# One of four weight sums on VectorE, fills begun several tasks ahead, first loads through one queue

## The chip, the core and the metric

The kernel runs on one core of one Trainium2 chip. Its time is device microseconds (us) of that core from launch to end. The kernel before was timed three times: 1735.0, 1737.59 and 1738.17 us, so the median is 1737.59 us. A further execution was taken with the hardware profiler; all rows in this document come from such executions.

The engines are named as in the profile: PE is TensorE's matrix multiply and PEld its weight load, DVE is VectorE, ACT is ScalarE, POOL is GpSimd, SP is the sync engine, which only issues DMAs here. ACT and POOL issue DMAs too.

## What is computed

One layer of a hybrid block on a sequence of 512 positions with 2048 channels, all in float32. Cut to what matters:

```
h = rmsnorm(x, norm_g)                       # (512, 2048)
proj = h @ w_in                              # (2048, 15360) weights: ten parts
a_u, a_b, a_c, a_z, b_v, b_g, b_z, c_u, c_z, gates = split(proj)
y_a = (silu(a_z) * a_b * conv3(a_c * a_u)) @ w_br_a
v   = conv31(b_v * sigmoid(b_g)) + conv_b    # causal, per channel, 31 taps
y_b = (silu(b_z) * silu(layernorm(v))) @ w_br_b
y_c = (silu(c_z) * (group(meanpool(c_u) - c_u) * scale)) @ w_br_c
merged = sigmoid(g0) * y_a + sigmoid(g1) * y_b + sigmoid(g2) * y_c
out = rmsnorm(x + merged @ w_o, final_g)
```

## The kernel before

**The product with w_in is done in 15 units.** A unit is a pair of 512-column blocks of `w_in`. Its two operands are cut in two by rows (channels 0-1023 and 1024-2047), in two by columns (the pair) and in two by positions (0-255 and 256-511), and the two-by-two block product is made with seven half-size products in place of eight. They are named `11`, `12`, `s1`, `s4`, `s2`, `s3`, `22`, in this order (the table `PRODUCTS`). Each of the seven has four *stages* of one weight block, 128 partitions x 1024 columns, 512 KB; so a unit has 28 stages and reads 28 blocks, 14 MB, of the 16 blocks of `w_in` that it uses. Every float32 number is split in a high part (`wh` for weights, made by ACT, L132) and a low part (`wl`, made by DVE, L133), and a product takes three matmuls: high x high, high x low, low x high.

**The weights of the seven products are sums.** In a unit, tile `rawA` of a stage is loaded with block (0,0) for `11`; for `s1` block (0,1) is added to it in place; for `s2` block (1,1) is added; for `22` block (1,0) is added. Tile `rawB` is loaded with block (1,0) for `12`; another `rawB` is loaded with block (1,1) for `s4`, and for `s3` block (0,1) is added to it. In the kernel before, each addition is an accumulating DMA that POOL issues (`accum_op`, L113): it reads the block from device memory and adds it to the tile. It waits until DVE has made `wl` of the tile's earlier content. Plain loads are issued by SP (L109). There are four `rawA` and six `rawB` tiles, so a plain load waits until the tile's earlier content has been split. The class `Weights` runs this: `next()` hands the matmuls a split block, `split_to` splits two stages ahead of them, `load_to` issues loads up to four stages ahead of the split.

**Other work is a list of tasks.** Vector work (31-tap convolution, layer norm, pooling, gates) is put in `todo` with a cost for each task; after the matmuls of every half stage (a step) `feed()` runs tasks until a credit of `rate` per step is used up. Results that are needed only later are spilled to device memory by a DMA that ACT issues (`spill`) and brought back by one that SP issues (`fill`); before the change most fills are tasks of cost 0 that stand one task, or a few, ahead of their use. Spilled and filled tiles, and nearly every temporary, share one pool of 20 buffers of 256 KB (`tp`). The recorded program is then put in an order for each engine by a scheduler that goes by its own timeline; the weight splits have a high priority in it (`AHEAD`).

**The start.** `x` is needed twice: transposed (`xT`, in 16 tiles of 128 x 2 x 256 floats) as the matmul operand, and by rows (`xn`, 16 tiles) for the sums of squares of the norm. The eight `xT` tiles of positions 0-255 (`xa` and `x12`) are loaded by DMAs that ACT issues, the eight of positions 256-511 by SP, in the steps of unit 0. Each `xn` tile is loaded by SP and squared by ACT in one call (`square`).

**The last part.** After the 15 units, the three branch products (w_br) and the product with `w_o` run in plain form: 80 more weight blocks with one load each.

The functions that the change touches, and what calls them, with the profile's line numbers:

Of the kernel before, what the change touches and what calls it, by code (L numbers as in the profile page):

```python
# [9 lines left out]
F32R = mybir.dt.float32r  # L10
AF = mybir.ActivationFunctionType
ALU = mybir.AluOpType
# [6 lines left out]
KB = WB // P  # L19
# [3 lines left out]
CONV_B = 31  # L23
# [5 lines left out]
RAW = 2 * CH  # L29
AHEAD = 300  # L30
WARM = 8


P_G = 0
# [11 lines left out]
for _c in (0, CH):  # L46
# [44 lines left out]
class Weights:  # L91
# [3 lines left out]
    def __init__(self, tc, nc, pools, parts, src, load_ahead, split_ahead):  # L95
        self.tc, self.nc, self.pools, self.parts, self.src = tc, nc, pools, parts, src
        self.load_ahead, self.split_ahead = load_ahead, split_ahead
        self.stages = stages()
        self.last = {s[1]: n for n, s in enumerate(self.stages)}
        self.raw, self.done = {}, {}  # L100
        self.loaded = self.split = self.at = 0

    def load_to(self, n):
        while self.loaded < min(n, len(self.stages)):
            tag, key, what, b = self.stages[self.loaded]
            if what == "load":
                t = self.pools[tag].tile([P, RAW], F32, tag=tag, name=f"raw{tag}{self.loaded}")
                for at in self.pieces(self.loaded):
                    self.nc.sync.dma_start(out=t[:, at], in_=self.src[b][:, at])  # L109
            else:  # L110
                t, before = self.raw[key]
                assert self.split > before
                self.nc.gpsimd.dma_start(out=t, in_=self.src[b], accum_op=ALU.add)  # L113
            self.raw[key] = t, self.loaded
            self.loaded += 1

    def pieces(self, n):
        step = CH if n == 0 else RAW
# [35 lines left out]
def trunk(ctx: ExitStack, tc: tile.TileContext, xT, xn, wts, par, fg, out):  # L154
# [85 lines left out]
    urgent, todo = deque(), deque()  # L240
    rate, credit = [0.5], [0.0]

    def add(cost, f, *args):
        todo.append((cost, lambda: f(*args)))

    def soon(cost, f, *args):
        urgent.append((cost, lambda: f(*args)))

    def feed():
        credit[0] = min(credit[0] + rate[0], 2.0)  # L250
        while credit[0] > 0.0 and (urgent or todo):
            cost, f = (urgent or todo).popleft()
            f()
            credit[0] -= cost

    def flush():
        while urgent or todo:
            (urgent or todo).popleft()[1]()

    def halves(src, t):  # L260

# [84 lines left out]

    squares = const.tile([P, 4 * NT], F32, name="squares")

    def square(t, c):
        x = tmp("xq")  # L350
        nc.sync.dma_start(out=x, in_=xn[t, :, c * CH : (c + 1) * CH])
        A.activation(out=x, in_=x, func=AF.Square, accum_out=squares[:, 4 * t + c : 4 * t + c + 1])

    def roots():
# [132 lines left out]
    def conv_tasks(i):  # L487
# [26 lines left out]
            else:  # L514
                V.tensor_tensor(out=csum[0], in0=csum[0], in1=c, op=ALU.add)

        return [(0.0, load), (0.5, first)] + [(0.7, lambda s=s: tap(s)) for s in range(1, CONV_B)] + [(0.7, last)]

    def pair_tasks(i):
        for pair in zip(conv_tasks(i), conv_tasks(i + 1)):  # L520
            todo.extend(pair)

    mean, var, rstd, held = {}, {}, {}, {}

# [3 lines left out]
    def center_tasks():  # L528
# [23 lines left out]
            var.clear()  # L552

        add(0.7, average)
        add(0.0, conv_load, 0)
        add(1.0, lambda: None)
        for i in range(KB):
            if i + 1 < KB:
                add(0.0, conv_load, i + 1)
            add(1.4, center, i)  # L560
        add(3.5, spread)

    def act_tasks():
# [19 lines left out]
        add(0.0, load, 0)  # L583
        for i in range(KB):
            if i + 1 < KB:
                add(0.0, load, i + 1)
            add(2.6, act, i)


# [59 lines left out]
    def pool_tasks(gi):  # L649
# [27 lines left out]
            ucd[2 * gi + o] = spill(s, "uc")  # L677

        mean_cost = 2.2 + 0.8 * gi
        add(0.0, load, "cu", cud, 0)  # L680
        add(0.0, load, "cu", cud, 1)
        add(mean_cost, mean_of, 0)
        add(0.0, weights)
        add(mean_cost, mean_of, 1)
        add(0.0, load, "cz", czd, 0)
        add(0.7, weights_split)
        add(0.0, load, "cz", czd, 1)
        add(1.0, lambda: None)
        add(0.7, mix, 0)
        add(0.7, mix, 1)  # L690
        add(0.0, st.clear)


    def halved(d, u, i):
        t = fill(d[i], "u")
        u[i] = halves(t, slot(F32R, "u"))

    def halved_tasks(d, u):
        for i in range(KB):
            add(0.7, halved, d, u, i)  # L700


    gd = [[[None] * 4 for _ in range(NT)] for _ in range(3)]
# [4 lines left out]
    def first_each(n):  # L708
        while makes and KD * len(sets) // 2 - 2 * len(makes) <= n + 4:
            make(*makes.popleft())  # L710
        if n in (2, 4, 6, 8):
            j = n // 2 - 1
            xload(nc.sync, x22[j], j, 1, 1)
            xload(nc.sync, xa[j][:, :, half[1]], j, 0, 1)
        if n == 10:
            nc.sync.dma_start(out=prm, in_=par)
        if n >= 32 and n % 3 == 2:
            square(*squares_left.popleft())

    def second_each(n):  # L720
        if n % 2 == 0 and squares_left:
            square(*squares_left.popleft())
        if n == 18:
            roots()
        if n >= 20 and late:
# [262 lines left out]
```

## Time and profile before

| | us |
|---|---|
| median of three runs | 1737.59 |
| the profiled execution, its own time | 1735.44 |
| its span, first to last instruction | 1733.7 |
| PE busy | 1658.1 |
| DVE busy | 1077.9 |
| ACT busy | 736.7 |
| POOL busy (issuing DMAs included) | 208.3 |
| mean granted TensorE clock, share of full speed | 0.986 |

The profiled execution took 1735.44 us, 1.7 us more than its span; the difference lies before the first and after the last instruction. Matmuls are pipelined, so PE can be busy and still not issue at its best rate: the number of matmuls in a stretch of time, shown in parentheses behind the busy time, says more than the busy time. A matmul of this kernel moves 512 columns, apart from some transposes of 128.

### The profile page before, as it was taken

The page shows a single profiled execution, that of the slowest core. Times are in us where ns is not written, and L with a number is a line of the kernel's source. Part 1 is how long each engine was busy: PE and PEld are TensorE (multiplying, and loading weights), DVE is VectorE, ACT ScalarE, POOL GpSimd, SP SyncE. Part 2 cuts the span into 40 slices and gives each one's busy share as a digit, 9 for nine tenths or more (in the row PEclk, how much of TensorE's full clock was granted, in tenths as well). Part 3 has the DMA queues.
Part 4 walks back from the last instruction along what each step waited for, and adds up shares of the span by engine and source line. Part 5 has one row for each costly group of instructions (what it writes and reads, how often), then busy time and mean ns, then how long its engine had stood idle before and what let it go on. Part 6 is the DMA issues. An engine that isn't in the chain of part 4 may idle for free.

```text
span 1733.7 us, 19754 instructions
## 1 busy us (share of the span) xinstructions
PE 1658.1 (96%) x7332; PEld 1355.1 (78%) x7332; DVE 1077.9 (62%) x1360; ACT 736.7 (42%) x919; POOL 208.3 (12%) x246
## 2 busy tenths in 40 slices
PE   5899999999999999999899989999899999999997
PEld 4677887887878787887687868888688888888887
DVE  5845699599679859756776754545543444553342
ACT  5645543443444454555554544545541211222222
POOL 0202020211112121212021102121200000000000
PEclk9999999999999999999999989999899999999999
DMA  9789897988879897989898989998995544443212
GB/s 314 145 226 208 241 193 183 196 203 200 184 186 201 201 231 177 240 216 277 249 258 244 276 244 210 226 206 245 223 297 184 195 146 146 134 146 92 91 37 97
DMA packets 119504, 345.41 MB, mean 199 GB/s; under 512 B 13168, under 2 KB 17392, under 8 KB 119408
## 3 DMA queue, kind: packets, MB, share of 16 engines
q0 software_dynamic: 34560, 125.84, 39.7%
q1 hardware_dynamic: 61216, 177.40, 31.0%
q10 hardware_dynamic: 23632, 40.91, 6.6%
q8 instruction: 57, 0.93, 0.2%
q14 instruction: 39, 0.32, 0.0%
HBM read 308.45 MB, written 35.65 MB: 198 GB/s over the span
## 4 chain that ended last, share of the span: by engine, by line
PE 83%; DMA 8%; DVE 4%; ACT 2%; issue 1%; SPq 0%; ACTq 0%; DVEq 0%
PE X L379 11%; PE X L380 10%; PE X L381 10%; PE Z L379 5%; PE Z L380 5%; PE Z L381 5%; PE y L816 5%; PE y L815 5%; PE y L814 5%; PE V L380 3%; PE V L379 3%; PE V L381 3%; PE o L888 3%; PE o L890 3%; PE o L889 3%; DVE wl L133 2%
## 5 line engine op out<-in xcount | busy, mean ns | idle before, releaser
L133 DVE TENSOR_TENSOR wl<-rawA,wh 128x1024 fp32r<-128x1024 f32 (+1 forms) x281 | 341.8, 1218 | 251.2 <-ACT wh L132 247.6
L132 ACT CAST wh<-rawA 128x1024 fp32r<-128x1024 f32 (+1 forms) x281 | 294.5, 1049 | 435.6 <-PE X L380 146.2
L133 DVE TENSOR_TENSOR wl<-rawB,wh 128x1024 fp32r<-128x1024 f32 x220 | 268.4, 1222 | 285.5 <-ACT wh L132 284.4
L132 ACT CAST wh<-rawB 128x1024 fp32r<-128x1024 f32 x220 | 231.2, 1053 | 343.8 <-PE y L815 106.5
L113 POOL DMA_DIRECT2D rawA<-wts x180 | 155.7, 865 | 902.8 <-DVE wl L133 865.0
L379 PE MATMUL X<-wh,x 128*128 128x512 f32 x480 | 191.5, 400 | 33.6 <-ACT x L307 17.3
L379 PE MATMUL X<-wh,xs 128*128 128x512 f32 x480 | 192.3, 401 | 20.0 <-ACT wh L132 18.1
L379 PE MATMUL Z<-wh,xs 128*128 128x512 f32 x480 | 189.4, 396 | 6.1 <-ACT wh L132 3.8
L380 PE MATMUL X<-wh,xs 128*128 128x512 f32 x480 | 190.2, 396 | 0.0
L380 PE MATMUL Z<-wh,xs 128*128 128x512 f32 x480 | 188.0, 392 | 2.3 <-DVE xs L300 2.3
L380 PE MATMUL X<-wh,x 128*128 128x512 f32 x480 | 189.7, 395 | 0.0
L381 PE MATMUL X<-wl,x 128*128 128x512 f32 x480 | 179.7, 397 | 0.0
L381 PE MATMUL X<-wl,xs 128*128 128x512 f32 x480 | 175.9, 397 | 3.8 <-DVE wl L133 3.7
L381 PE MATMUL Z<-wl,xs 128*128 128x512 f32 x480 | 174.1, 392 | 0.1
L502 DVE SCALAR_TENSOR_TENSOR conv<-v,prm,conv 128x511 f32<-128x511 f32 (+28 forms) x240 | 165.6, 726 | 0.1
L814 PE MATMUL y<-wh,u 128*128 128x512 f32 x384 | 149.9, 390 | 0.0
L815 PE MATMUL y<-wh,u 128*128 128x512 f32 x384 | 149.7, 390 | 0.0
L816 PE MATMUL y<-wl,u 128*128 128x512 f32 x384 | 149.5, 390 | 0.0
L379 PEld LDWEIGHTS X<-wh,x 128*128 128x128 f32 x480 | 91.7, 191 | 59.2 <-issue 17.7
L379 PEld LDWEIGHTS X<-wh,xs 128*128 128x128 f32 x480 | 91.7, 191 | 46.8 <-ACT wh L132 20.0
L379 PEld LDWEIGHTS Z<-wh,xs 128*128 128x128 f32 x480 | 90.4, 189 | 32.6 <-ACT snap L387 7.2
L381 PEld LDWEIGHTS X<-wl,xs 128*128 128x128 f32 x480 | 91.6, 192 | 25.3 <-DVE wl L133 5.9
(172 smaller groups left out, 2289.3 us busy)
## 6 DMA issues: line engine op xcount, KB each, us to landing
rawA<-wts POOLq DMA_DIRECT2D x180, 512.0 KB, 7.5
rawB<-wts SPq DMA_DIRECT2D x160, 512.0 KB, 5.2
rawA<-wts SPq DMA_DIRECT2D x99, 512.0 KB, 4.1
rawB<-wts POOLq DMA_DIRECT2D x60, 512.0 KB, 7.7
g<-g SPq DMA_DIRECT2D x48, 256.0 KB, 5.2
d<-turn ACTq DMA_DIRECT2D x32, 256.0 KB, 7.0
g<-gate ACTq DMA_DIRECT2D x24, 256.0 KB, 6.0
g<-snap ACTq DMA_DIRECT2D x24, 256.0 KB, 5.6
```

The source lines that it names most:

```text
L113: self.nc.gpsimd.dma_start(out=t, in_=self.src[b], accum_op=ALU.add)
L132: self.nc.scalar.copy(out=h[:, at], in_=raw[:, at])
L133: self.nc.vector.tensor_tensor(out=l[:, at], in0=raw[:, at], in1=h[:, at].bitcast(F32), op=ALU.subtract)
L379: T.matmul(p, lhsT=xh, rhs=h, start=start and k == 0, stop=False, skip_group_check=True)
L380: T.matmul(p, lhsT=xl, rhs=h, start=False, stop=False, skip_group_check=True)
L381: T.matmul(p, lhsT=xh, rhs=l, start=False, stop=k == KB - 1, skip_group_check=True)
L502: V.scalar_tensor_tensor(out=c[:, s:], in0=v[:, : S - s], scalar=pcol(P_BW, i * CONV_B + CONV_B - 1 - s), in1=c[:, s:], op0=ALU.mult, op1= ...
L814: T.matmul(banks[t], lhsT=uh[:, tk], rhs=h, start=k == 0, stop=False)
L815: T.matmul(banks[t], lhsT=ul[:, tk], rhs=h, start=False, stop=False)
L816: T.matmul(banks[t], lhsT=uh[:, tk], rhs=l, start=False, stop=k == KB - 1)
L888: T.matmul(pt[t], lhsT=mh[:, tk], rhs=h, start=k == 0, stop=False)
L889: T.matmul(pt[t], lhsT=ml[:, tk], rhs=h, start=False, stop=False)
```

## The change

1. **The sum for `s2` moves from a DMA to VectorE.** The block that `s2` adds to `rawA`, (1,1), is the one that `s4` has loaded in `rawB`. The entry of `s2` in the table becomes `sum`, and `sum_to` issues a `tensor_tensor` add of the two tiles on DVE, with the priority of the splits. 60 of the 240 accumulating DMAs go, and 60 adds of 128 x 1024 float32 come. The next sum on the `rawB` tile (for `s3`) may start only once the add has read it.
2. **Fills begin ahead.** `before(f)` files a load with the planned cost of the tasks ahead of it, and `begin_loads` starts it when the tasks done are within `LOAD_AHEAD` = 7.0 cost units of it. An empty task of 7.0 units is put behind the layer norm's statistics.
3. **The squares' loads** start two squares ahead of the squaring.
4. **The first loads** all go through SP, weight block and `xT` tile in turn; the second half of `xT` follows at once and is no longer spread over unit 0's steps.

```diff
-    ("s2", "A", "add", 1, 1),
+    ("s2", "A", "sum", 1, 1),
...
     def load_to(self, n):
...
+            if what == "sum":
+                pass
...
+    def sum_to(self, n):
+        while self.summed < min(n, len(self.stages)):
+            _, key, what, b = self.stages[self.summed]
+            if what == "sum":
+                t, before = self.raw[key]
+                assert self.split > before and self.loaded > self.summed
+                with self.tc.high_priority(AHEAD):
+                    self.nc.vector.tensor_tensor(out=t, in0=t, in1=self.held[b], op=ALU.add)
+                self.raw[key] = t, self.summed
+            self.summed += 1
...
     def split_to(self, n):
         while self.split < min(n, len(self.stages)):
             n_stage = self.split
+            self.load_to(n_stage + 1)
+            self.sum_to(n_stage + 3)
             self.load_to(n_stage + 1 + self.load_ahead)
...
-    w.load_to(1)
     for j in range(STEPS):
-        xload(nc.scalar, xa[j][:, :, half[0]], j, 0, 0)
+        w.load_to(j + 1)
+        xload(nc.sync, xa[j][:, :, half[0]], j, 0, 0)
     for j in range(STEPS):
-        xload(nc.scalar, x12[j], j, 1, 0)
+        w.load_to(STEPS + j + 1)
+        xload(nc.sync, x12[j], j, 1, 0)
+    for j in range(STEPS):
+        xload(nc.sync, x22[j], j, 1, 1)
+        xload(nc.sync, xa[j][:, :, half[1]], j, 0, 1)
...
+    def before(f, *args):
+        loads.append((planned[0], lambda: f(*args)))
...
+    def begin_loads():
+        while not urgent and loads and loads[0][0] <= spent[0] + LOAD_AHEAD:
+            loads.popleft()[1]()
...
-        add(0.0, conv_load, 0)
         add(1.0, lambda: None)
         for i in range(KB):
-            if i + 1 < KB:
-                add(0.0, conv_load, i + 1)
+            before(conv_load, i)
             add(1.4, center, i)
         add(3.5, spread)
+        add(LOAD_AHEAD, lambda: None)
...
-        if n >= 32 and n % 3 == 2:
-            square(*squares_left.popleft())
+        if n >= 24 and n % 3 == 2:
+            square_load()
+            if n >= 32:
+                square(*xqs.popleft())
```

The loads of the convolution's `v`, the activation's `c` and `z`, the pooling's `cu`, `cz` and weights, and the branches' `u` are turned from tasks into `before(...)` in the same way.

How this moves instructions shows at three places. The first is SP's queue at the start; the rows are its loads from the first on, before the change (`rawA0` is stage 0's block, the number behind `raw` is the stage):

```order
L109 DMA rawA0_93<-wts 128x512 x2
L109 DMA rawA1_162<-wts 128x1024
L109 DMA rawA2_164<-wts 128x1024
L109 DMA rawA3_166<-wts 128x1024
L109 DMA rawB4_168<-wts 128x1024
L109 DMA rawB5_176<-wts 128x1024
L109 DMA rawB6_182<-wts 128x1024
L205 DMA xa_1_81<-xT 128x2x256
L205 DMA x22_9_89<-xT 128x2x256
L109 DMA rawB7_207<-wts 128x1024
L205 DMA x22_10_90<-xT 128x2x256
```

and with it:

```order
L113 DMA rawA0_93<-wts 128x512 x2
L228 DMA xa_1_81<-xT 128x2x256
L113 DMA rawA1_97<-wts 128x1024
L228 DMA xa_2_82<-xT 128x2x256
L113 DMA rawA2_100<-wts 128x1024
L228 DMA xa_3_83<-xT 128x2x256
L113 DMA rawA3_103<-wts 128x1024
L228 DMA xa_4_84<-xT 128x2x256
L113 DMA rawB4_106<-wts 128x1024
L228 DMA x12_5_85<-xT 128x2x256
L113 DMA rawB5_109<-wts 128x1024
L228 DMA x12_6_86<-xT 128x2x256
```

The `xT` tiles `xa_1` to `xa_4` and `x12` were on ACT's queue and now stand in SP's, each behind its stage's block; the `x22` tiles and the second halves of `xa`, which began ahead of block 7, moved behind it.

The second is DVE in unit 6, in the product `s1` (stages 176 to 179) and the first stages of `s4` (180 on); `conv` are taps of the convolution, `snap` joins of products. Before:

```order
L133 TENSOR_TENSOR wl177_4030<-rawA169_3751,wh177_4029 128x1024
L502 SCALAR_TENSOR_TENSOR conv_207_3763<-v_205_3747,prm_104,conv_207_3763 128x497
L392 TENSOR_TENSOR snap_220_3965<-V_222_3969,snap_220_3965 128x512
L502 SCALAR_TENSOR_TENSOR conv_206_3749<-v_204_3745,prm_104,conv_206_3749 128x496
L392 TENSOR_TENSOR snap_221_3966<-V_223_3970,snap_221_3966 128x512
L133 TENSOR_TENSOR wl178_4058<-rawA170_3780,wh178_4057 128x1024
L502 SCALAR_TENSOR_TENSOR conv_207_3763<-v_205_3747,prm_104,conv_207_3763 128x496
L502 SCALAR_TENSOR_TENSOR conv_206_3749<-v_204_3745,prm_104,conv_206_3749 128x495
L133 TENSOR_TENSOR wl179_4077<-rawA171_3799,wh179_4076 128x1024
L502 SCALAR_TENSOR_TENSOR conv_207_3763<-v_205_3747,prm_104,conv_207_3763 128x495
L133 TENSOR_TENSOR wl180_4096<-rawB180_4008,wh180_4095 128x1024
```

and with the change, where `rawA168<-rawA168,rawB180` is a sum for `s2`:

```order
L556 SCALAR_TENSOR_TENSOR conv_207_3763<-v_199_3599,prm_126,conv_207_3763 128x497
L446 TENSOR_TENSOR snap_220_3965<-V_222_3969,snap_220_3965 128x512
L446 TENSOR_TENSOR snap_221_3966<-V_223_3970,snap_221_3966 128x512
L134 TENSOR_TENSOR rawA169_3751<-rawA169_3751,rawB181_4027 128x1024
L156 TENSOR_TENSOR wl178_4058<-rawA170_3780,wh178_4057 128x1024
L556 SCALAR_TENSOR_TENSOR conv_206_3749<-v_198_3597,prm_126,conv_206_3749 128x496
L156 TENSOR_TENSOR wl179_4077<-rawA171_3799,wh179_4076 128x1024
L556 SCALAR_TENSOR_TENSOR conv_207_3763<-v_199_3599,prm_126,conv_207_3763 128x496
L156 TENSOR_TENSOR wl180_4095<-rawB180_4008,wh180_4094 128x1024
L134 TENSOR_TENSOR rawA170_3780<-rawA170_3780,rawB182_4055 128x1024
L556 SCALAR_TENSOR_TENSOR conv_206_3749<-v_198_3597,prm_126,conv_206_3749 128x495
L134 TENSOR_TENSOR rawA171_3799<-rawA171_3799,rawB183_4074 128x1024
```

The four sums stand among the low parts of `s1` and the first of `s4`, ahead of the low part of the `rawB` block that they read.

The third is SP's queue around the fills of the activation (`c` and `z`), in unit 11, before:

```order
L191 DMA c_526_7357<-cd_370_5985 128x512
L191 DMA z_527_7359<-d_336_5787 128x512
L191 DMA c_528_7361<-cd_373_6010 128x512
L191 DMA z_529_7363<-d_339_5796 128x512
L109 DMA rawB340_7854<-wts 128x1024
L191 DMA c_532_7420<-cd_382_6060 128x512
L191 DMA z_533_7422<-d_342_5805 128x512
L109 DMA rawB341_7872<-wts 128x1024
L191 DMA c_542_7497<-cd_385_6091 128x512
L191 DMA z_543_7499<-d_345_5814 128x512
L191 DMA c_548_7553<-cd_390_6131 128x512
L191 DMA z_549_7555<-d_348_5823 128x512
```

and with the change:

```order
L113 DMA rawB340_7838<-wts 128x1024
L113 DMA rawB341_7856<-wts 128x1024
L214 DMA c_532_7490<-cd_374_5993 128x512
L214 DMA z_533_7492<-d_338_5791 128x512
L214 DMA c_534_7494<-cd_377_6018 128x512
L214 DMA z_535_7496<-d_341_5800 128x512
L214 DMA c_536_7498<-cd_386_6068 128x512
L214 DMA z_537_7500<-d_344_5809 128x512
L214 DMA c_538_7502<-cd_388_6096 128x512
L214 DMA z_539_7504<-d_347_5818 128x512
L214 DMA c_544_7564<-cd_392_6133 128x512
L214 DMA z_545_7566<-d_350_5827 128x512
```

The first two pairs of `c` and `z` stood ahead of block 340 and the third between it and block 341; now the first seven pairs, of which five are shown, stand in one piece behind block 341.

## Rows read from the trace of the kernel before

**Rows 1.** The page: busy time by engine; DMA queues with packets, MB, share.

```profile
PE 1658.1 (96%) x7332; PEld 1355.1 (78%) x7332; DVE 1077.9 (62%) x1360; ACT 736.7 (42%) x919; POOL 208.3 (12%) x246
...
q0 software_dynamic: 34560, 125.84, 39.7%
q1 hardware_dynamic: 61216, 177.40, 31.0%
```

**Rows 2.** Windows: length, busy (instructions) by engine, PEclk, DMA share, GB/s.

```profile
0.00:22.20 22.20, 3.79 (x16) 3.49 (x16) 4.69 (x23) 5.25 (x8) 3.43 (x9) 1.00 0.95 294
22.20:118.00 95.80, 86.67 (x344) 67.94 (x345) 68.36 (x106) 58.35 (x99) 12.90 (x15) 0.95 0.83 213
118.00:196.00 78.00, 75.99 (x330) 61.20 (x329) 42.77 (x50) 43.81 (x61) 13.02 (x16) 1.00 0.89 212
...
780.00:1060.00 280.00, 261.12 (x1116) 211.20 (x1115) 186.89 (x247) 139.02 (x169) 42.76 (x50) 0.97 0.95 256
...
1200.00:1300.00 100.00, 91.80 (x386) 74.08 (x385) 49.51 (x52) 46.92 (x59) 10.35 (x12) 0.95 0.93 260
```

**Rows 3.** Window of steady matmuls, same columns.

```profile
1320.00:1340.00 20.00, 20.00 (x90) 16.54 (x90) 7.63 (x8) 4.00 (x4) 0.00 (x0) 1.00 0.45 137
```

**Rows 4.** Chain that ended last: start, length, what.

```profile
811.87 8.04 DMA c<-cd
...
827.38 10.01 DMA cu<-d
...
919.92 6.66 DMA cu<-d
...
1005.67 13.41 DMA c<-cd
...
1230.61 19.61 DMA u<-uc
```

**Rows 5.** Windows of the late stalls, columns as Rows 2.

```profile
820.00:860.00 40.00, 32.31 (x130) 25.07 (x129) 30.19 (x40) 20.90 (x26) 3.45 (x4) 0.91 0.87 252
920.00:940.00 20.00, 17.13 (x75) 13.57 (x74) 16.77 (x33) 9.51 (x12) 0.00 (x0) 1.00 0.81 276
1000.00:1040.00 40.00, 32.68 (x131) 25.72 (x130) 21.10 (x24) 18.54 (x22) 3.45 (x4) 0.87 0.88 242
1220.00:1260.00 40.00, 32.00 (x123) 24.86 (x123) 22.37 (x27) 20.03 (x28) 7.61 (x9) 0.87 0.93 216
```

**Rows 6.** Timeline of ACT at the start: start, length, what, [idle before <-releaser].

```profile
3.55 0.62 ACT L132 CAST wh<-rawA 128x512 fp32r<-128x512 f32 x1
5.21 0.62 ACT L132 CAST wh<-rawA 128x512 fp32r<-128x512 f32 x1 [1.05 <-DMA rawA<-wts]
...
16.24 1.04 ACT L132 CAST wh<-rawA 128x1024 fp32r<-128x1024 f32 x1 [6.88 <-DMA xa<-xT]
21.14 0.38 ACTq L205 DMA_DIRECT2D x<-xT  x1
...
21.67 2.49 ACT L307 ACTIVATE x<-xa,gcol 128x256 fp32r<-128x256 f32 x6
```

**Rows 7.** Timeline of PE at the start.

```profile
22.21 1.22 PE L379 MATMUL X<-wh,x 128*128 128x512 f32 x2 [17.30 <-ACT x L307]
```

**Rows 8.** Tile xq: idle until, us in total, times.

```profile
  DMA xq<-xn: 16.2, 7
```

**Rows 9.** The page: low parts by DVE, busy us, mean ns.

```profile
L133 DVE TENSOR_TENSOR wl<-rawB,wh 128x1024 fp32r<-128x1024 f32 x220 | 268.4, 1222 | 285.5 <-ACT wh L132 284.4
```

**Rows 10.** Plain weight loads (L109): issue to landing.

```profile
DMA to landing us min/median/max: 2.7/4.5/12.9
```

**Rows 11.** Windows of the convolution, columns as Rows 2.

```profile
200.00:300.00 100.00, 97.82 (x435) 79.87 (x434) 91.14 (x117) 42.41 (x48) 14.70 (x17) 0.98 0.86 208
500.00:600.00 100.00, 96.63 (x425) 78.72 (x424) 94.91 (x124) 44.57 (x49) 13.84 (x16) 0.98 0.83 201
600.00:700.00 100.00, 98.49 (x464) 81.27 (x463) 76.76 (x92) 50.31 (x63) 17.28 (x20) 1.00 0.87 203
```

More of the change, by code (lines that the diff above doesn't have):

```diff
@@ L31 @@
 WARM = 8
+LOAD_AHEAD = 7.0
 P_G = 0
@@ L99, in __init__ @@
         self.last = {s[1]: n for n, s in enumerate(self.stages)}
-        self.raw, self.done = {}, {}
-        self.loaded = self.split = self.at = 0
+        self.first_sum = {s[3]: n for n, s in enumerate(self.stages) if s[2] == "sum"}
+        self.raw, self.raw_of, self.held, self.done = {}, {}, {}, {}
+        self.loaded = self.summed = self.split = self.at = 0
     def load_to(self, n):
@@ L105, in load_to @@
             tag, key, what, b = self.stages[self.loaded]
-            if what == "load":
+            if what == "sum":
+                pass
+            elif what == "load":
                 t = self.pools[tag].tile([P, RAW], F32, tag=tag, name=f"raw{tag}{self.loaded}")
@@ L112, in load_to @@
                 assert self.split > before
+                first = self.first_sum.get(self.raw_of[key], -1)
+                assert first < self.summed
                 self.nc.gpsimd.dma_start(out=t, in_=self.src[b], accum_op=ALU.add)
-            self.raw[key] = t, self.loaded
-            self.loaded += 1
+            if what == "load":
+                self.raw_of[key] = b
+                self.held[b] = t
+            if what != "sum":
+                self.raw[key] = t, self.loaded
+            self.loaded += 1
+    def sum_to(self, n):
[8 more added lines that the diff above has]
+            self.summed += 1
     def pieces(self, n):
@@ L347, in trunk, with square_load, square @@
     squares = const.tile([P, 4 * NT], F32, name="squares")
-    def square(t, c):
-        x = tmp("xq")
-        nc.sync.dma_start(out=x, in_=xn[t, :, c * CH : (c + 1) * CH])
+    xqs = deque()
+    def square_load():
+        if squares_left:
+            t, c = squares_left.popleft()
+            x = tmp("xq")
+            nc.sync.dma_start(out=x, in_=xn[t, :, c * CH : (c + 1) * CH])
+            xqs.append((t, c, x))
+    def square(t, c, x):
         A.activation(out=x, in_=x, func=AF.Square, accum_out=squares[:, 4 * t + c : 4 * t + c + 1])
@@ L515, in last @@
                 V.tensor_tensor(out=csum[0], in0=csum[0], in1=c, op=ALU.add)
-        return [(0.0, load), (0.5, first)] + [(0.7, lambda s=s: tap(s)) for s in range(1, CONV_B)] + [(0.7, last)]
+        before(load)
+        return [(0.5, first)] + [(0.7, lambda s=s: tap(s)) for s in range(1, CONV_B)] + [(0.7, last)]
     def pair_tasks(i):
         for pair in zip(conv_tasks(i), conv_tasks(i + 1)):
-            todo.extend(pair)
+            for task in pair:
+                add(*task)
     mean, var, rstd, held = {}, {}, {}, {}
@@ L581, in act @@
                 rstd.clear()
-        add(0.0, load, 0)
         for i in range(KB):
-            if i + 1 < KB:
-                add(0.0, load, i + 1)
+            before(load, i)
             add(2.6, act, i)
@@ L679, in pool_tasks, with load, halved @@
         mean_cost = 2.2 + 0.8 * gi
[L680 to L685, printed above, removed]
+        for ct in range(2):
+            before(load, "cu", cud, ct)
+            add(mean_cost, mean_of, ct)
+        before(weights)
         add(0.7, weights_split)
-        add(0.0, load, "cz", czd, 1)
         add(1.0, lambda: None)
-        add(0.7, mix, 0)
-        add(0.7, mix, 1)
+        for o in range(2):
+            before(load, "cz", czd, o)
+            add(0.7, mix, o)
         add(0.0, st.clear)
-    def halved(d, u, i):
-        t = fill(d[i], "u")
-        u[i] = halves(t, slot(F32R, "u"))
     def halved_tasks(d, u):
+        raw = {}
+        def load(i):
+            raw[i] = fill(d[i], "u")
+        def halved(i):
+            u[i] = halves(raw.pop(i), slot(F32R, "u"))
         for i in range(KB):
-            add(0.7, halved, d, u, i)
+            before(load, i)
+            add(0.7, halved, i)
     gd = [[[None] * 4 for _ in range(NT)] for _ in range(3)]
@@ L710, in first_each @@
             make(*makes.popleft())
[L711 to L715, printed above, removed]
+        if n == 4:
             nc.sync.dma_start(out=prm, in_=par)
-        if n >= 32 and n % 3 == 2:
-            square(*squares_left.popleft())
+        if n >= 24 and n % 3 == 2:
+            square_load()
+            if n >= 32:
+                square(*xqs.popleft())
     def second_each(n):
-        if n % 2 == 0 and squares_left:
-            square(*squares_left.popleft())
+        if n % 2 == 0:
+            square_load()
+            if xqs:
+                square(*xqs.popleft())
         if n == 18:
```

18 lines of the change are left out of this document (14 added, 4 removed).

## Prediction

> **What bounds the kernel now.** I read the page's busy times first. PE is busy for 96% of the span, DVE for 62% [rows 1]; the time is TensorE's, and only what stops or slows TensorE can be won or lost. Busy time hides slow matmuls, so the second view is a table of windows with the count of matmuls. Where nothing is waited for, 90 matmuls start in 20 us [rows 3], 0.222 us each. A stretch of t us could hold 4.5 t of them; what is missing, times 0.222 us, is what the stretch lost by waits and by a lower clock together. By that sum the stretch before the first matmul is 22.2 us; unit 0 holds 344 of 431 and loses 19.3 us; unit 1 holds 330 of 351 and loses 4.7 us; from 780 to 1060 us 1116 of 1260 (32 us), and from 1200 to 1300 us 386 of 450 (14.2 us) [rows 2]. The convolution in between loses little: 435 of 450 and 425 of 450 in its worst two windows [rows 11].
>
> The third view is the chain that ended last. In the late losses it leaves TensorE and runs through DMAs, and always through fills: c, cu, c, u, at 8.0, 10.0, 6.7, 13.4 and 19.6 us each [rows 4]. The windows around them hold 130 of 180, 75 of 90, 131 of 180 and 123 of 180 matmuls, so they lost 11.1, 3.3, 10.9 and 12.7 us, 38 us in all, part of it at a granted clock of 0.87 to 0.91 after the wait [rows 5]. The fills are slow because the DMA engines are full: shares of 0.95 and 0.93 there [rows 2].
>
> The fourth view is the start. ScalarE has the first weights at 3.55 and 5.21 us, waits for an x tile until 16.24 us, has another x load in its own queue until 21.14 us, scales the first x tile at 21.67 us [rows 6], and TensorE starts at 22.21 us [rows 7].
>
> **The change part by part.** The sum is made against the profiled execution, 1735.4 us, which is 2.2 us below the median of the runs, 1737.6 us; no correction is made for that.
>
> *Sums.* What they take from the DMA engines: the accumulating queue holds 39.7% of sixteen engines' time for 240 transfers [rows 1], so one costs 0.397 x 1733.7 / 240 = 2.87 us of all sixteen. 60 fewer free 172 us. A unit has 12 left of 16 (34 us of some 77), so its DMA share falls by 4 x 2.87 / 77, or 0.15: from 0.95 to about 0.80 late. Spare time for fills goes from a twentieth to a fifth. What they put on DVE: an add of two 128x1024 tiles, taken as the low part's row of the same shape and type, 1222 ns [rows 9]; 60 make 73 us, 4.9 us a unit. Late, DVE is busy 187 of 280 us and 50 of 100 [rows 2]; there the adds are covered. In the convolution DVE is busy 91 and 95 of 100 us in the dense windows and 77 in a slack one [rows 11]. If an add pushes a join of a product back, TensorE waits. Bounds: four dense units at 4.9 us, +20 us, if nothing gives; −6 us if half of the some 12 us that the two dense windows and others lose goes, since the v fills come earlier. I take +2 us, near the lower end: the order has the sums in s1 and s4, and fewer taps beside them, while joins that TensorE waits for stand at the end of s3.
>
> *Start.* The first plain loads cost 0.310 x 1733.7 / 177.4 = 3.03 us a MB [rows 1], 0.8 us for a 256 KB x tile, 1.6 us for a block. The second half of block 0 landed by 5.2 us [rows 6]; the x tile now stands right behind it, so some 6.0 us, and the matmul follows the first scaling by 0.54 us (21.67 to 22.21) [rows 6, 7]: 6.5 us, 15.7 us earlier. ScalarE no longer holds x loads. Not all of unit 0 follows: the first eight blocks and eight x tiles (6.3 MB, 19 us), then 2.1 MB of x (6.4 us), with four accumulates for s1 (11.5 us) beside them, are needed by the end of s1; that is 37 us of DMA, about what 12 stages of matmuls take (33 us) plus the start. Then DVE stops at the first sum until block 12 has landed, some 42 us, and behind that sum stand the operands of s4 and the last of s1. I take unit 0's loss as 14.4 in place of 19.3 us. What goes of it is the wait of ScalarE for squares, 16.2 us in 7 places [rows 8], now loaded two ahead; what comes is the DMA limit. Sum of start and unit 0: −15.7 − 4.9 = −20.6 us. Bounds: −28 us (half of unit 0's loss goes) and −8 us (unit 0 gives half of the start back).
>
> The Trainium skill speaks against this part: in DMA: Bandwidth & Descriptors, Issuing engines are not separate DMA queues, it says that loads of any queue run on the same 16 DMA engines and that spreading them over several saves issue time alone. By that, gathering the x loads in SP's queue would bring nothing, and the start would stay. The rows show sixteen engines at 0.95 up to 22.2 us [rows 2], so the engines are indeed the limit; but they moved seven weight blocks, of which two were needed, and an x tile late. The same page, Queues, rings and completion order, says that an engine takes turns between queues; so two queues share, and one keeps its order. The sum by the first rule alone is rival D.
>
> *Fills.* A load now begins up to 7 cost units ahead, 14 steps of 1.36 us (six matmuls) or 19 us, against 6.7 to 19.6 us of landing [rows 4]. That hides a fill only if SP's queue lets it out; a load behind a weight block that waits for its buffer starts no earlier. The order shows both: the center's c fills moved forward by up to six stages' loads, but the u fills still stand behind the same block, and seven pairs of c and z behind block 341. There the freed DMA time does the work: 16 u fills need 12.7 us of DMA, the four accumulates no longer in that window needed 11.5. I take 8 of 11.1 us, 2.5 of 3.3, 7.5 of 10.9 and 6 of 12.7: −24 us. Bounds: −36 us, nearly all, and −8 us if only the c fills that moved gain. The 20 buffers are held longer; SP may wait for one, with weight blocks behind it, and I hold that inside the bound. Spills, w_br and w_o are left as they are: no DMA wait is in the steady window [rows 3]. The empty task only delays the pooling, which has two units of slack: no cost.
>
> Sum: 1735.4 − 20.6 + 2 − 24 = 1692.8 us.
>
> **The rivals.**
>
> B, the fills stay late. For it: SP's order for u, c and z, and 0.95 of DMA share that only falls to 0.80. Against it: the center's fills did move. Start −20.6, convolution +4, late −6: 1713 us.
>
> C, nearly everything goes: start −26, late −36, convolution 0: 1673 us. For it: every late chain runs through a fill, and the slow clock goes with the wait. Against it: SP's order.
>
> D, the page's rule on queues: bytes ahead of the first matmul set the start, not their order; start 0, late −24, convolution +2: 1713 us. Against it: block 0 had landed at 5.2 us, and only x was missing.
>
> E, the other side: the sum becomes the wait. It stands in DVE's order ahead of low parts of s1 and of s4, and it needs a rawB block that the old order needed only some three stages later. If the block lands late, DVE stops, the next low part is late, and TensorE with it. A block of s4 gets its buffer when a low part of the second product is made, five stages or 13.6 us before the sum that needs it; plain blocks land in 4.5 us (median), 12.9 us at most [rows 10]. The point is a landing of some 13 us, where fills in bursts hold SP's queue. To eat the gain of 43 us it takes 2.9 us a unit in 15 units; at 3.5 us it is +10: 1745 us. Against it: the median leaves 9 us, and there are fewer bytes.
>
> A sixth, small: gains and losses cancel within 0.2%.
>
> **How the numbers follow.** My forecast 0.50, B 0.19, C 0.13, D 0.06, E 0.09, cancelling 0.03. Predicted: 1693 us. The likeliest case's own range is 1680 to 1706 us. The range for 8 in 10 runs from C's time, 1673, past B's and D's 1713 to 1724, the sum with both gains near their small ends (−11 and −9) and +9 in the convolution; E and the rest stay out. What a measurement of this kernel can tell from no change is about 0.2%, 3.5 us. Faster by more: A, B, C and D, 0.88; within: 0.03; slower: 0.09.
>
> **What the profile of the changed kernel would show.** Right: the first matmul at 6 to 8 us, and the waits of ACT for xq gone; 180 accumulating DMAs with some 30% of the engines' time; 60 adds of 1.2 us on DVE; DMA share near 0.80 from 780 us on; windows of 40 us in the pooling and activation with at least 160 matmuls; no DMA of c or cu over 5 us in the chain. Wrong: if DVE's idle time ends at a rawB landing before a sum, E is at work; if the chain still runs through u or c for 10 us, B; if the first matmul comes after 15 us, D; if the dense convolution windows hold under 400 matmuls in 100 us, the adds cost far more than I took. If unit 0 alone loses over 25 us, the DMA limit at the start was sized too small.

## The result and the profile after

The changed kernel takes 1708.99 us (median of 4 runs, 1707.05 to 1712.01); the ratio to the kernel before is 0.9839, with a 95% interval of 0.9819 to 0.986. The forecast was 1693 us, in a range of 1673 to 1724 us; the time lies in that range, and outside the likeliest case's own, 1680 to 1706 us. The profiled execution took 1707.05 us, its span 1705.3 us, 28.4 us less than before. The page shows what the sums moved; the columns are those of [rows 1]:

```profile
PE 1651.0 (97%) x7332; PEld 1348.6 (79%) x7332; DVE 1140.5 (67%) x1420; ACT 736.4 (43%) x919; POOL 156.9 (9%) x186
...
q1 hardware_dynamic: 63392, 179.50, 31.7%
q0 software_dynamic: 25920, 94.38, 30.5%
```

DVE has 60 instructions and 62.6 us more, POOL 60 DMAs fewer, and the accumulating queue went from 39.7% to 30.5% of the engines' time. The next rows answer to [rows 2], [rows 5] and [rows 11], with the same windows and columns:

```profile
0.00:22.20 22.20, 15.73 (x64) 12.10 (x64) 10.25 (x32) 10.36 (x16) 4.31 (x10) 1.00 0.93 255
22.20:118.00 95.80, 81.84 (x325) 63.88 (x326) 70.31 (x103) 58.97 (x102) 10.35 (x12) 0.93 0.80 222
118.00:196.00 78.00, 75.36 (x339) 60.59 (x338) 46.13 (x53) 42.42 (x55) 9.52 (x11) 1.00 0.71 173
200.00:300.00 100.00, 97.40 (x433) 78.98 (x432) 97.35 (x124) 40.77 (x44) 11.27 (x13) 1.00 0.71 181
...
500.00:600.00 100.00, 95.82 (x420) 78.02 (x420) 96.77 (x121) 43.18 (x49) 11.28 (x13) 0.98 0.68 169
600.00:700.00 100.00, 98.55 (x465) 81.29 (x464) 83.00 (x100) 51.59 (x65) 13.01 (x15) 1.00 0.76 188
780.00:1060.00 280.00, 271.27 (x1178) 220.91 (x1177) 209.96 (x269) 145.52 (x175) 33.94 (x39) 0.99 0.85 235
...
820.00:860.00 40.00, 39.80 (x174) 32.32 (x174) 29.83 (x37) 24.30 (x30) 3.49 (x4) 1.00 0.98 282
920.00:940.00 20.00, 20.00 (x90) 16.57 (x89) 13.27 (x21) 9.44 (x12) 3.48 (x4) 1.00 0.87 255
1000.00:1040.00 40.00, 35.09 (x148) 28.32 (x148) 24.52 (x28) 16.73 (x19) 3.46 (x4) 0.96 0.83 246
1220.00:1260.00 40.00, 39.80 (x175) 32.33 (x174) 19.39 (x20) 20.00 (x23) 2.39 (x3) 1.00 0.91 251
```

Three of the four late stalls are gone: 174 matmuls for 130, 90 for 75, 175 for 123, with the granted clock back at 1.00; the third kept about two thirds of its loss (148 for 131, of 180). The start is the other story. By 118 us TensorE has done 389 matmuls for 360, a lead of 29 matmuls or 6.4 us, although its first matmul came 15.1 us earlier than in [rows 7]. PE's waits in the timeline show where the rest went at first:

```profile
7.10 0.73 PE L433 MATMUL X<-wh,x 128*128 128x512 f32 x2 [2.19 <-ACT x L354]
...
16.78 0.73 PE L433 MATMUL X<-wh,x 128*128 128x512 f32 x2 [0.75 <-ACT x L354]
25.66 1.22 PE L433 MATMUL V<-wh,x 128*128 128x512 f32 x2 [5.78 <-ACT x L354]
```

The product `12` (tile `V`) stands still for 5.8 us, because ACT waits for the x tile.

For all kernels together, one number says most: the **gain by stretch**, the matmuls that a kernel starts in a stretch less those that the kernel before starts there, divided by 4.5 per us. The counts come from windows 0 to 40, 40 to 100, 100 to 200, 200 to 780 and 780 to 1300 us of one profiled execution each (before: 85, 209, 426, 2560, 2108). The stretches are the load limit at the start, the rest of unit 0, unit 1, the convolution, and the late units. A lead is the sum of the gains up to a time; the texts set down before the runs quote it from finer windows, which differ by some tenths of a us. Each ratio is to executions of the kernel before that were timed together with the kernel (medians 1736.4 to 1737.9 us). The profiled execution can lie some us off the median: those of kernels 8 and 9, 1700.9 and 1709.9 us, are the slowest of their five.

| kernel | median us | ratio, 95% | 0-40 | 40-100 | 100-200 | 200-780 | 780-1300 |
|---|---|---|---|---|---|---|---|
| the change | 1709.0 | 0.9839 (0.9819-0.986) | 6.0 | -2.4 | 2.9 | -4.2 | 25.3 |
| 1 no sums | 1707.5 | 0.9828 (0.9813-0.9843) | 6.4 | 1.3 | 1.8 | 0.2 | 16.2 |
| 2 old start | 1719.9 | 0.9896 (0.988-0.9911) | 0.7 | -0.7 | -11.3 | -5.1 | 29.6 |
| 3 no loads ahead | 1713.6 | 0.9866 (0.9847-0.9884) | 6.0 | -3.3 | 0.2 | -4.9 | 24.2 |
| 4 sums from unit 10 | 1700.3 | 0.9794 (0.9771-0.9816) | 6.0 | 0.2 | 0.4 | 0.7 | 25.1 |
| 5 neither sums nor ahead | 1723.6 | 0.9926 (0.9903-0.995) | 6.0 | -0.4 | 4.0 | 0.2 | 3.1 |
| 6 as 4, accumulates wait | 1702.3 | 0.9803 (0.9776-0.983) | 6.2 | -3.3 | 2.2 | 1.3 | 26.4 |
| 7 squares not ahead | 1712.7 | 0.9859 (0.9831-0.9887) | 6.0 | -3.8 | -1.8 | -4.9 | 25.6 |
| 8 as 4, plain blocks for s1 | 1696.8 | 0.977 (0.9755-0.9785) | 9.1 | -2.0 | -1.1 | 1.8 | 25.6 |
| 9 sums from unit 1 | 1706.3 | 0.9828 (0.9813-0.9842) | 6.4 | 0.7 | -2.2 | -5.1 | 24.9 |
| 10 as 8, squares in unit 1 | 1692.3 | 0.9744 (0.9717-0.9771) | 9.1 | 3.1 | 3.6 | 1.8 | 26.7 |

### The profile page after: what moved, and what is told of

It reads as the page before. It is cut to its first block, busy times and chain, and to the rows that moved or that the text cites. A ratio compares the mean times of both kernels' runs of the same rounds, so it can differ in the third digit from the quotient of the medians.

```text
span 1705.3 us, 19733 instructions
## 1 busy us (share of the span) xinstructions
PE 1651.0 (97%) x7332; PEld 1348.6 (79%) x7332; DVE 1140.5 (67%) x1420; ACT 736.4 (43%) x919; POOL 156.9 (9%) x186
## 3 DMA queue, kind: packets, MB, share of 16 engines
q0 software_dynamic: 25920, 94.38, 30.5%
## 4 chain that ended last, share of the span: by engine, by line
PE 84%; DVE 6%; issue 2%; ACT 1%; DMA 1%; ACTq 0%; SPq 0%; DVEq 0%
PE X L433 11%; PE X L434 11%; PE X L435 11%; PE Z L433 5%; PE Z L435 5%; PE y L872 5%; PE y L870 5%; PE y L871 5%; PE Z L434 5%; PE o L944 3%; PE o L946 3%; PE o L945 3%; DVE wl L156 2%; PE V L433 2%; PE V L434 2%; PE V L435 2%
## 5 line engine op out<-in xcount | busy, mean ns | idle before, releaser
L433 PE MATMUL X<-wh,x 128*128 128x512 f32 x480 | 188.4, 395 | 17.7 <-DVE snap L446 14.8
L433 PE MATMUL X<-wh,xs 128*128 128x512 f32 x480 | 189.3, 395 | 1.9 <-ACT xs L346 1.7
L434 PE MATMUL X<-wh,x 128*128 128x512 f32 x480 | 188.2, 392 | 0.1
L434 PE MATMUL X<-wh,xs 128*128 128x512 f32 x480 | 187.5, 391 | 0.0
L556 DVE SCALAR_TENSOR_TENSOR conv<-v,prm,conv 128x485 f32<-128x485 f32 (+14 forms) x240 | 167.4, 732 | 0.1
L119 POOL DMA_DIRECT2D rawA<-wts x120 | 104.1, 868 | 567.0 <-DVE wl L156 553.3
L435 PEld LDWEIGHTS Z<-wl,xs 128*128 128x128 f32 x480 | 90.1, 189 | 27.7 <-DVE wl L156 9.2
```

What stands on the lines that cost most here:

```text
L433: T.matmul(p, lhsT=xh, rhs=h, start=start and k == 0, stop=False, skip_group_check=True)
L434: T.matmul(p, lhsT=xl, rhs=h, start=False, stop=False, skip_group_check=True)
L435: T.matmul(p, lhsT=xh, rhs=l, start=False, stop=k == KB - 1, skip_group_check=True)
L556: V.scalar_tensor_tensor(out=c[:, s:], in0=v[:, : S - s], scalar=pcol(P_BW, i * CONV_B + CONV_B - 1 - s), in1=c[:, s:], op0=ALU.mult, op1= ...
```

## The experiments

**1. No sums on VectorE.**

```diff
-    ("s2", "A", "sum", 1, 1),
+    ("s2", "A", "add", 1, 1),
```

> The changed kernel with the sums of s2 as accumulating DMAs again (240 of them), the rest of the change kept. Theory 1: the sums cost TensorE some 5 us in unit 0, where DVE has no idle time from 40 to 75 us, and some 5 us in the convolution, and by the DMA time that they free they give about half of the late gain. So about 10 us come back before 780 us, and some 15 to 20 of the 27 us won after it are lost: 1712 to 1720 us. Rival 2, the loads that begin ahead won the late stretch alone: about 1699 us. Rival 3, the freed DMA time won it alone: 1724 us or more, with the chain through c, cu and u fills of over 6 us again.

Measured: 1707.5 us; the interval overlaps that of the change, so the sums as a whole bring nothing that can be told. They are two effects that cancel: without them the convolution is 4.4 us better and 40 to 100 us is 3.7 us better, and the late units are 9.1 us worse. The chain that ended last then runs through a `u` fill again:

```profile
1205.14 13.89 DMA u<-uc
```

The lower end of theory 1 was some 5 us too high, because the loads ahead alone keep 16.2 us of the late gain, more than I took.

**2. The start as before.** The first half of the x loads goes to ACT's queue again and the second half to unit 0's steps (with the load of `prm`, the parameters, from step 4 to step 10; that part of the edit is left out below).

```diff
+    w.load_to(1)
     for j in range(STEPS):
-        w.load_to(j + 1)
-        xload(nc.sync, xa[j][:, :, half[0]], j, 0, 0)
+        xload(nc.scalar, xa[j][:, :, half[0]], j, 0, 0)
     for j in range(STEPS):
-        w.load_to(STEPS + j + 1)
-        xload(nc.sync, x12[j], j, 1, 0)
-    for j in range(STEPS):
-        xload(nc.sync, x22[j], j, 1, 1)
-        xload(nc.sync, xa[j][:, :, half[1]], j, 0, 1)
+        xload(nc.scalar, x12[j], j, 1, 0)
...
```

> The changed kernel with the first loads as they were before (x on ACT's queue, the second half of x in unit 0's steps). Theory 1: the start won 15 us for the first matmul, but what came after is limited by DMA and DVE, so that only some 6 to 7 us are left at 200 us; without it the time is 1714 to 1718 us. Rival 2, the start's 15 us are all in the time, and the sums in unit 0 took another 8 us: 1722 to 1726 us. Rival 3, the matmuls that start early are worth nothing in the end, since unit 0 ends by DVE's work: 1709 us.

Measured: 1719.9 us, between the two theories, and the table says why it settles neither: 5.3 us are missing by 40 us, as theory 1 has it, but the largest loss, 14.2 us against the change, is in unit 1, where one square's tile lands late and TensorE waits behind it. The row is of the chain that ended last:

```profile
117.80 16.02 DMA xq<-xn
```

So the undo of the start disturbs the squares too; it does not isolate one term.

**3. No loads ahead.**

```diff
-LOAD_AHEAD = 7.0
+LOAD_AHEAD = 0.0
```

> The changed kernel with LOAD_AHEAD = 0, so that a fill is begun one task ahead as before and the empty task costs nothing. Theory 1: loads ahead and freed DMA time each give about half of the 27 us won after 780 us: 1719 to 1726 us, with DMA fills of c, cu or u over 6 us in the chain again. Rival 2, the loads ahead give nearly all: 1730 to 1736 us. Rival 3, the freed DMA time alone: 1707 to 1713 us.

Measured: 1713.6 us, near rival 3. The late units keep 24.2 of 25.3 us. With the sums in place, loads ahead are hardly needed there. The 4.6 us between the medians are not certain, since the intervals overlap; in the profile most of the difference stands from 40 to 200 us (a loss of 3.1 us for a gain of 0.4).

**5. Neither sums nor loads ahead**, run to see whether the two stand in for each other (both edits above).

> The changed kernel with all sums as accumulating DMAs and LOAD_AHEAD = 0: the new start and the squares' loads ahead are all that is left of the change. Theory 1: loads ahead (16.6 us after 780 us with accumulating DMAs) and freed DMA time (25.8 us with LOAD_AHEAD = 0) each stand in for the other, so that without both the late stretch loses as before: a lead of 5 to 9 us at 780 us and about the same at 1300 us, 1727 to 1733 us. Rival 2, the late gain comes from something else that is still in this kernel (the start's other order of work): a lead of 20 us or more at 1300 us, 1712 to 1718 us.

Measured: 1723.6 us, a little below theory 1. The late gain falls to 3.1 us, and the long fills of [rows 4] are back in the chain:

```profile
946.31 7.20 DMA c<-cd
992.22 13.94 DMA c<-cd
...
1216.74 19.25 DMA u<-uc
```

So in the late units: neither 3.1 us, loads ahead alone 16.2, freed DMA time alone 24.2, both 25.3. The two are substitutes; their single gains do not add.

**4. Sums only where the convolution is over.**

```diff
             key = (u, tag, name == "12")
+            if what == "sum" and u < 10:
+                what = "add"
```

> The changed kernel with the sums on VectorE only from unit 10 on (about 780 us, where the convolution is over); units 0 to 9 add by DMA as before. Theory 1: unit 0 gets back about 5 us and the convolution about 5 us, the late stretch stays: 1697 to 1702 us. Rival 2, what was lost in unit 0 is the limit of the DMA engines and the drift in the convolution has another cause: 1706 to 1712 us.

Measured: 1700.3 us, as theory 1 has it, and faster than the change beyond both intervals. Of theory 1's two halves only the convolution's lasts in the profile: 4.9 us of the 5.1 us between the two profiled executions. Unit 0's 2.6 us (40 to 100 us) are gone by 200 us, where the lead is 6.7 us for the change's 6.4. The convolution (200 to 780 us) shows it in one row each, first the change:

```profile
200.00:780.00 580.00, 567.03 (x2541) 461.73 (x2540) 499.51 (x598) 262.32 (x299) 73.70 (x85) 1.00 0.72 178
```

and then this kernel:

```profile
200.00:780.00 580.00, 570.87 (x2563) 466.29 (x2562) 473.03 (x572) 266.00 (x302) 97.72 (x113) 1.00 0.87 206
```

28 DMAs on POOL stand against 26.5 us of DVE; the DMA engines' share is 0.87 for 0.72, and TensorE starts 22 matmuls more. There DMA time is not what is short.

**9. Only unit 0's sums undone** (`u < 1` in the same edit).

> The changed kernel with only unit 0's sums for s2 as accumulating DMAs again. Theory 1: the four adds stand in a stretch where DVE has no idle time and cost TensorE 3 to 5 us there; the sums of units 1 to 9 cost the other half of the 8.7 us by which the kernel with sums from unit 10 on is faster: 1703 to 1706 us, with a lead at 100 us of 6.5 to 8 us. Rival 2, the sums in unit 0 are all of it: 1700 us. Rival 3, they cost nothing in the end: 1709 us.

Measured: 1706.3 us, at the upper end of theory 1, with a lead of 7.1 us at 100 us; but the interval overlaps that of the change, so rival 3 is not excluded. In place the effect is plain. From 40 to 68 us the change has

```profile
40.00:68.00 28.00, 21.41 (x78) 15.80 (x79) 28.00 (x47) 18.59 (x36) 3.43 (x4) 0.92 0.53 149
```

and this kernel

```profile
40.00:68.00 28.00, 24.86 (x99) 19.37 (x100) 28.00 (x52) 20.47 (x38) 5.16 (x6) 0.94 1.05 260
```

DVE has no idle time in either, and 21 matmuls or 4.7 us are missing where DVE does the four adds, listed for the change from 42 to 70 us as

```profile
L134 DVE TENSOR_TENSOR rawA<-rawA,rawB 128x1024 f32<-128x1024 f32 x4 | 4.9, 1220 | 0.0
```

By 200 us, however, the change has 6.4 us of lead and this kernel 4.9: the difference is taken back in unit 1, where ACT waits longer for squares (20.5 us in all for 12.4); that this is the cause is not shown. How much of the 4.7 us stays in the end is left open.

**6. The accumulating DMAs of s1 made to wait**, on the kernel of experiment 4. `self.gate` holds the `x12` tiles; an add of one column on POOL reads the tile of the same number first.

```diff
+                if self.loaded < 3 * STEPS:
+                    g = self.gate[self.loaded - 2 * STEPS]
+                    self.nc.gpsimd.tensor_tensor(
+                        out=self.scratch, in0=t[:, :1], in1=g[:, 0, :1], op=ALU.add
+                    )
                 self.nc.gpsimd.dma_start(out=t, in_=self.src[b], accum_op=ALU.add)
...
```

> The kernel with sums from unit 10 on (1700.3 us), and in addition each of the first four accumulating DMAs of s1 waits until the x12 tile of the same number has landed (a one-column GpSimd add reads the tile and that x12 tile first). Theory 1: from 12 to 26 us the accumulating DMAs take DMA time that the loads for the second product need, and TensorE runs dry for 4 to 6 us there; with the wait the loads come first, the lead at 40 us over the kernel before rises from 6.4 to 9 to 12 us, and 3 to 5 us stay in the end: 1695 to 1697 us. Rival 2, bytes alone set the time at which s1 can start, and what is won at 26 us is lost again at 40 us: 1699 to 1702 us. Rival 3, the accumulating DMAs come too late for s1: 1703 us or more.

Measured: 1702.3 us; rival 2 is right and theory 1 wrong. The second product now runs through (85 matmuls from 8 to 28 us, 52 in the change), and then `s1` waits. Its first matmul comes as late as in the change:

```profile
40.05 0.74 PE L433 MATMUL Z<-wh,xs 128*128 128x512 f32 x2 [1.43 <-ACT xs L346]
```

and in this kernel

```profile
39.74 0.79 PE L442 MATMUL Z<-wh,xs 128*128 128x512 f32 x1 [9.10 <-ACT wh L162]
```

This kernel's windows from 28 us on:

```profile
28.00:32.00 4.00, 2.64 (x12) 1.86 (x10) 0.00 (x0) 0.00 (x0) 0.00 (x0) 1.00 1.05 242
32.00:36.00 4.00, 0.00 (x0) 0.00 (x0) 1.95 (x5) 2.46 (x6) 0.00 (x0) 0.82 1.09 369
36.00:40.00 4.00, 0.26 (x1) 0.26 (x2) 4.00 (x10) 3.64 (x7) 0.00 (x0) 0.50 1.04 406
40.00:44.00 4.00, 1.81 (x4) 0.90 (x4) 4.00 (x9) 2.08 (x3) 0.00 (x0) 0.50 1.02 405
```

At 40 us the gain is 6.2 us, the same as everywhere (6.0 to 6.4) in the eight kernels with the new start and accumulating DMAs for `s1`. The other seven begin their first loads in one order, so this is one other order tried: it moved the stall and won nothing by 40 us, with the same DMA work ahead of `s1`.

**8. The sums of s1 in unit 0 from plain loads**, on the kernel of experiment 4. The blocks of stages 8 and 9 are loaded ahead of the first and the second pair of tiles of the second half of x, those of 10 and 11 later; the other two pairs move to steps 9 and 11 and the load of `prm` to step 14 (left out below).

```diff
+                if self.loaded < 3 * STEPS:
+                    o = self.other.pop(self.loaded, None)
+                    if o is None:
+                        o = self.plain(self.loaded)
+                    with self.tc.high_priority(AHEAD):
+                        self.nc.vector.tensor_tensor(out=t, in0=t, in1=o, op=ALU.add)
+                else:
+                    self.nc.gpsimd.dma_start(out=t, in_=self.src[b], accum_op=ALU.add)
...
+    def plain(self, n):
+        o = self.pools["B"].tile([P, RAW], F32, tag="B", name=f"other{n}")
+        self.nc.sync.dma_start(out=o, in_=self.src[self.stages[n][3]])
+        return o
...
```

> The kernel with sums from unit 10 on, and the four sums of s1 in unit 0 made in another way: the second block is loaded plainly into a rawB tile, ahead of the second half of x or between it, and DVE adds it; no accumulating DMA is left before unit 0's s2. Theory 1: all kernels with the new start have the same lead of 6.0 to 6.7 us at 40 us because s1 waits for a given DMA time (8 blocks, 16 x tiles, 4 accumulating DMAs). Four plain blocks of 1.6 us in place of four accumulating DMAs of 2.87 us take 5.1 us of it, and DVE has idle time before 36 us for the adds: the lead at 40 us rises to 10 to 12 us, and 3 to 5 us stay: 1695 to 1697 us. Rival 2, DVE's work from 40 to 75 us sets the end of unit 0 whatever comes before: a higher lead at 40 us and none at 100 us, 1699 to 1703 us.

Measured: 1696.8 us, the time of theory 1 and 3.5 us below experiment 4; but these two intervals overlap, and the profile looks more like rival 2. The gain at 40 us is 9.1 us for 6.0, a little under what was expected; at 100 us the lead is 7.1 us for experiment 4's 6.2, and at 200 us 6.0 for 6.7. So the gain up to 40 us is shown, and whether it lasts is not. The last two columns of the windows (DMA share, GB/s) say why it comes about; the change first:

```profile
16.00:20.00 4.00, 3.12 (x13) 2.10 (x12) 0.89 (x2) 0.91 (x2) 0.86 (x1) 1.00 1.06 243
20.00:24.00 4.00, 0.00 (x0) 0.00 (x0) 1.23 (x1) 1.04 (x1) 0.00 (x0) 0.83 1.08 241
24.00:28.00 4.00, 2.34 (x6) 1.88 (x7) 1.43 (x3) 2.90 (x6) 0.00 (x0) 0.50 1.03 381
```

and with plain loads:

```profile
16.00:20.00 4.00, 4.00 (x19) 3.30 (x19) 3.10 (x4) 2.84 (x6) 0.00 (x0) 1.00 1.05 387
20.00:24.00 4.00, 4.00 (x20) 3.30 (x19) 2.56 (x6) 3.55 (x6) 0.00 (x0) 1.00 1.05 377
24.00:28.00 4.00, 4.00 (x19) 3.34 (x18) 4.00 (x8) 2.31 (x6) 0.00 (x0) 1.00 1.08 365
```

The engines are full in both, but with accumulating DMAs among the loads they move 241 to 243 GB/s, and without them 377 to 387.

**7. The squares' loads as before.**

```diff
-        if n >= 24 and n % 3 == 2:
-            square_load()
             if n >= 32:
+                square_load()
                 square(*xqs.popleft())
```

> The changed kernel with each square of unit 0 loaded just before it is squared, as before (n >= 32 for load and square). Theory 1: the loads two ahead did not take the waits away (12.4 us of idle ACT for xq in place of 16.2 us), and in the SP queue they wait 15.4 us for a buffer while the DMA engines are idle from 48 to 58 us; undone, unit 0 gains 1 to 4 us there and ACT waits some 4 us more in unit 1: 1706 to 1711 us. Rival 2, the prediction's step: the loads ahead are worth some 5 us in unit 0, and without them the time is 1712 to 1716 us. Rival 3, the idle DMA engines are the whole loss of 10 us from 40 to 70 us: 1699 to 1702 us.

Measured: 1712.7 us, where rival 2 has it; but the intervals of this and of the change overlap, so the 3.7 us between the medians are not certain. ACT's waits for the tile `xq` were 16.2 us in [rows 8], 17.2 us here, and in the change still

```profile
  DMA xq<-xn: 12.4, 6
```

**10. All squares in unit 1**, on the kernel of experiment 8.

```diff
-        if n >= 24 and n % 3 == 2:
+        if n in (50, 53):
             square_load()
-            if n >= 32:
-                square(*xqs.popleft())
...
-        if n == 18:
+        if n == 33:
             roots()
-        if n >= 20 and late:
+        if n >= 35 and late:
```

> The kernel before it (plain blocks for s1 in unit 0, sums from unit 10 on, 1696.8 us), with all 16 squares in unit 1, one at every second half stage, their loads still two ahead, and the root of the norm 15 half stages later. Theory 1: ACT waits 17.8 us for the squares' tiles in that kernel, in two stretches (84 to 100 us and 118 to 124 us), and TensorE loses some 8 us of matmuls there; with the squares spread in unit 1, where DVE and ACT have room, 3 to 6 us come back: 1691 to 1694 us. Rival 2, the loads of the squares stand behind weight blocks in SP's queue in unit 1 too, and ACT waits as long: 1696 to 1699 us.

Measured: 1692.3 us, within theory 1 and the lowest of all, though its interval still overlaps that of experiment 8 by a little. In place the effect is larger: 40 to 200 us gains 6.7 us against a loss of 3.1 us in experiment 8. Its reason is only half right: ACT still waits 15.8 us for squares (17.8 there), and TensorE loses less behind it. The squares of unit 1 were not tried without the plain blocks.

## Why the prediction was right or wrong

**Direction and size.** Faster, as forecast; 28.4 us of the 42.6 us. The 14.2 us that are missing are as much as the start and unit 0 fell short (6.4 us in place of 20.6). From 118 us on the kernel won 22.0 us, the 24 less 2 of the forecast; that this agrees so well is partly luck: a loss in the convolution 2.2 us larger than forecast met 2 us of gain in unit 1 (339 matmuls for 330) that was not forecast. The time lies next to the 1713 us of rivals B and D. B's mechanism did not happen: the fills did not stay late.

**Start and unit 0, -20.6 us: the step that failed.** Its first half was right: the first matmul at 7.10 us (6.5 forecast), no x load on ACT. Its second half was not: unit 0 was to lose 14.4 us after the first matmul, and by 118 us it lost 28.0: 373 matmuls (389 less 16 of the start) where 110.9 us hold 499. That is past the 25 us by which the prediction itself would call its DMA limit too small. The gain by 118 us is 6.4 us, below my smallest bound of 8. I had the 37 us of DMA work in the text and set it beside 33 us of matmuls, as if they could run side by side. But `s1` needs nearly all of it: its first matmul comes at 40.05 us, and what starts early waits later. Experiment 6 shows that the stall moves with the order of the loads and that nothing is won by it. Experiment 8 shows 3.1 us more by 40 us when four accumulating DMAs become plain loads; their order changed with it, so the two are not told apart. I had also put the adds at nothing in unit 0, where DVE has no idle time from 40 to 68 us and four adds of 1.22 us cost 4.7 us in place. And I took the squares' wait as gone; 12.4 of 16.2 us were left. Experiment 10 shows that much of it can be moved off the path.

The order of the loads did win the first 15.1 us, with rawA and xa in turn. By the Trainium skill (DMA: Bandwidth & Descriptors, Issuing engines are not separate DMA queues) loads interleave on the same 16 engines whatever engine starts them. The trace agrees: up to 40 us the engines moved 307 GB/s before, with the x loads on the queues of ACT and SP, and 303 GB/s with all of them on SP's (the last column).

```profile
0.00:40.00 40.00, 21.57 (x85) 18.01 (x86) 19.05 (x48) 19.58 (x34) 4.29 (x10) 1.00 0.99 307
```

and the change:

```profile
0.00:40.00 40.00, 28.70 (x112) 22.38 (x112) 22.12 (x51) 22.82 (x38) 4.31 (x10) 0.91 0.99 303
```

At the same rate the new order still won 6.0 us by 40 us (112 matmuls for 85), and experiment 2, with the old order, has 5.3 us less.

**Convolution, +2 us.** It is +4.2 us, within the bounds of -6 to +20. The five kernels with sums there lose 4.2 to 5.1 us, and the six without gain 0.2 to 1.8: on the mean -4.8 against 1.0, so about 6 us for the sums of the units in that stretch. Fewer taps beside the adds were not enough cover; DVE is busy 97.35 and 96.77 of 100 us in the dense windows.

**Fills, -24 us.** Measured 25.3 us from 780 to 1300 us. By place I forecast 8, 2.5, 7.5 and 6 us; it was 9.8, 3.3, 3.8 and 11.6, with small losses elsewhere. Most of the stall near 1000 us stayed, with `c` fills still behind a weight block, as the order had shown, and a row over the 5 us that the prediction named as its sign:

```profile
992.48 8.95 DMA c<-cd
```

The `u` fills stood behind their block too, and yet their stall went. That the freed DMA time would do the work there was right, and experiments 3 and 5 show it: 24.2 us by that alone, with 0.85 of DMA share for 0.95.

**Rivals.** E, the sum waiting for its rawB block, did not happen: the 60 adds have almost no idle time ahead of them.

```profile
L134 DVE TENSOR_TENSOR rawA<-rawA,rawB 128x1024 f32<-128x1024 f32 x60 | 73.1, 1221 | 0.5
```

Their price is the time that they take on a full DVE, not a wait. D is out as it was put, since the first matmul came at 7.10 us; but its parts (0, +2 and -24 us) are the nearest to the measured -6.4, +4.2 and -25.3, because the DMA work up to `s1`, and not up to the first matmul, took most of the start's gain. C is out: its start of -26 us and its late -36 us were both too large.

## What to carry to other kernels

An earlier first matmul was worth here only what the first stage that needs nearly every early load allowed: add up the DMA time up to that stage, accumulating transfers at their own price, before booking the gain. Move a sum from a DMA to an engine stretch by stretch, where DMA is full and the engine is not; done everywhere it gave back here what it won, and from unit 10 on it was 8.7 us better by the medians, 5.1 us by the profiled executions. Two cures for one wait should be tried alone before their gains are added.

## What the runs showed of the hardware

Accumulating DMAs beside plain ones lowered what full engines moved, by the bytes that the profile counts: 241 to 243 GB/s in the change against 377 to 387 GB/s in experiment 8, both from 16 to 24 us at a busy share of 1.05 to 1.08. After TensorE had stood still from about 30 to 39.7 us in experiment 6, the granted clock was 0.50 in the windows from 36 to 44 us, the lower of its two levels (1.2 GHz), while matmuls had begun again.
